# Five of eleven weight chunks of a down projection by seven block products in place of eight

## The chip, the core and the metric

The kernel runs on one core of one Trainium2 chip. The metric is the device time of one execution in microseconds (us), the median of several runs; lower is better. The core's engines are named as in the profile: PE is TensorE's matmul, PEld its weight load, DVE VectorE, ACT ScalarE, POOL GpSimd, SP the engine that issues most transfers. Each runs its own instructions in the order written, and waits where another has not finished.

## The reference

One decoder layer over 256 tokens of width 1024: two groups of attention heads, an output projection, a layer norm, a feed-forward block, a second layer norm. What matters here is the end of it, in float32:

```python
h = _layer_norm(ALPHA * h + mix_out, ln1_g[l], ln1_b[l])
gate = jnp.einsum('bsd,df->bsf', h, w_gate[l])
up = jnp.einsum('bsd,df->bsf', h, w_up[l])
ffn = jnp.einsum('bsf,fd->bsd', jax.nn.silu(gate) * up, w_down[l])
h = _layer_norm(ALPHA * h + ffn, ln2_g[l], ln2_b[l])
```

With `D_FF` = 2816, the down projection `w_down` is a product of 256 x 2816 by 2816 x 1024.

## The kernel before, in words

**Precision.** Every float32 operand of a big product is split in two parts of a type that TensorE takes in one pass: ACT copies the rounded high part, DVE subtracts it for the low part (`split`, L75). `prod` (L177) then issues three matmuls for one product: high by high, high by low, low by high. Nearly all matmuls and splits stand at L68, the helper that records them; the tile names tell them apart.

**Weights.** They come in chunks of 128 x 2048 (1 MB). The class `Weights` (L79) loads each with one transfer into a ring of four raw buffers (`wraw`) and splits it into a ring of `NSPLIT` = 5 pairs (`whi`, `wlo`). A chunk can be split once the matmuls that read the pair five places before are done. `piece` splits the next slice; `get` splits what is still missing of a chunk; `free` gives a pair back.

**Feed-forward.** 22 groups f of 128 features. From f = 3 on `ff_by_channel` (L566) issues 48 matmuls of 256 columns per group (tile `pg`), then ACT takes the silu of the gate half, DVE multiplies by the up half, and the product is split into the two tiles `a` that the down projection reads. Between the matmuls, `Order.fill` (L380) hands out a piece of 512 columns of the next weights each time its own count of time passes `PACE`.

**Down projection** (L605 to L641). Eleven chunks c of two feature groups each. The activations are stationary (128 x 128), the weights move. Token block t = 0 is summed in two banks of 512 columns, t = 1 in three, of 512, 256 and 256 columns (`thirds`), all named `d`. The first seven chunks go through all five banks one after the other: per chunk 18 matmuls of 512 columns and 12 of 256. After each, two pieces of 1024 columns of a later chunk are split. The last four chunks (`nlast`) are gone through bank by bank in `finish` (L631): first the two banks of t = 0, whose layer norm then runs on DVE, then the three of t = 1. `layer_norm` (L490) adds the residual `x_nat` times ALPHA to each bank, takes statistics, normalises and stores.

PSUM has eight banks, in four tags of two: `big`, `o`, `in`, `sml`. Neither rule of order is written by hand to the instruction: a scheduler orders each engine's instructions between what must wait for what.

Of the kernel before, what the change touches and what calls it, by code (L numbers as in the profile page):

```python
# [10 lines left out]
F32 = mybir.dt.float32  # L11
# [24 lines left out]
NWARM = 7  # L36
ALPHA = 2.0 ** 0.25
# [7 lines left out]
def decoder_layer(ctx: ExitStack, tc: tile.TileContext, first, x, wqk, wv, wo, wgu, wd,  # L45
# [33 lines left out]
    class Weights:  # L79


        def __init__(self, chunks):
            self.chunks = chunks
            self.raw, self.parts = [], []
            self.pos = 0
            self.freed = 0

        def load(self, n=NRAW):

            while len(self.raw) < min(n, len(self.chunks), len(self.parts) + NRAW - (self.pos % 2048 > 0)):  # L90
# [5 lines left out]

        def piece(self, width):

            c, o = divmod(self.pos, 2048)
            if c == len(self.chunks):  # L100
                return False
            if o == 0:
                if c - self.freed >= NSPLIT:
# [12 lines left out]
        def get(self, c, width=512):  # L116
            while self.pos < (c + 1) * 2048:
                assert self.piece(width)
            return self.parts[c]

        def free(self, c):
            self.freed = max(self.freed, c + 1)
# [37 lines left out]
    for h in range(2):  # L160
# [4 lines left out]
                       *(wo[c] for c in range(4)), *(wgu[f] for f in range(NFF)), *(wd[c] for c in range(NFF // 2))])  # L165
# [193 lines left out]
    class Order:  # L359
        def __init__(self):  # L360
            self.now = 0.0
            self.steps = []
            self.since = 0.0

# [19 lines left out]
        def fill(self, cost, fn):  # L384
# [4 lines left out]
            while self.since >= PACE:  # L389
                self.since -= PACE  # L390
# [99 lines left out]
    def layer_norm(acc, res, g, b, dst, after, pieces, after_pieces=None):  # L490
# [4 lines left out]
        for i, c in enumerate(pieces):  # L495
            nc.vector.scalar_tensor_tensor(y[:, c], res[:, c], ALPHA, acc[i][:, :c.stop - c.start],
# [69 lines left out]
    def ff_by_channel(f, tag):  # L566
        w = weights.get(14 + f, 1024)
        act_tiles(f)
        p = bank(tag, "pg")
        for half in range(2):  # L570
            for kt in range(KT):
                c = slice(kt * 256 + half * 128, kt * 256 + half * 128 + 128)
                od.fill(0.33, lambda: prod(p[:, half * 256:half * 256 + 256], (w[0][:, c], w[1][:, c]),
                                           (xhi[:, kt, :], xlo[:, kt, :]), kt == 0, kt == KT - 1))
        weights.free(14 + f)
        a = gated(p[:, 0:256], p[:, 256:512], [128, 256], "aw")
        split(a, *act[f])
# [22 lines left out]
    for f in range(NX, NFF):  # L600
        ff_by_channel(f, ("in", "sml")[f % 2])
# [6 lines left out]
    accd = [[bank(tag, f"d{t}") for tag in tags] for t, tags in enumerate((("big", "big"), ("o", "sml", "in")))]  # L608

    def down(t, f, i, w):  # L610
        tk = slice(t * 128, t * 128 + 128)
        p = pieces[t][i]
        c = slice((f % 2) * 1024 + p.start, (f % 2) * 1024 + p.stop)
        ah, al = act[f]
        prod(accd[t][i][:, :p.stop - p.start], (ah[:, tk], al[:, tk]), (w[0][:, c], w[1][:, c]),
             f == 0, f == NFF - 1)
# [94 lines left out]
```

## Time and profile before

| | us |
|---|---|
| median of 3 runs (lowest, highest) | 322.66 (322.24, 324.42) |
| the profiled execution | 322.32 |
| its span, first to last instruction | 320.6 |
| PE busy in the span | 310.2 (97%) |
| DVE busy | 206.1 (64%) |
| ACT busy | 176.6 (55%) |
| down projection, matmuls on the chain that ended last | 61.23 |

The span is what the trace covers; the execution's own time is 1.7 us longer. Matmul rows overlap in the trace, since each is shown from its start to its modelled end: the rate of TensorE is read from the distance between starts, not from the length of a row. In a timeline, a row with x2 stands for two instructions merged.

### The profile page before, as it was taken

Reading aid. Unit: us, or ns where it says so; the run is one execution under the profiler, and the core shown is the slowest. Engines: PE = TensorE matmul, PEld = TensorE weight load, DVE = VectorE, ACT = ScalarE, POOL = GpSimd, SP = SyncE. Lnnn points to the kernel's source line nnn. Section 1 sums busy time; section 2 is a strip of 40 time slices with the busy share of each in tenths; the row PEclk is TensorE's granted clock in tenths of the full one; section 3 lists DMA queues with packets and bytes.
Section 4 is the critical chain, followed back from the end, with each engine's and each line's share of the span. In section 5 each row is a group of like instructions: output and inputs, shape, how many; then the busy total and the mean of one; then the engine's idle time right before and its main releaser. Section 6 shows DMA issues by size and latency. Waiting matters only on the chain.

```text
span 320.6 us, 5490 instructions
## 1 busy us (share of the span) xinstructions
PE 310.2 (97%) x2175; PEld 283.3 (88%) x2175; DVE 206.1 (64%) x422; ACT 176.6 (55%) x385; POOL 4.1 (1%) x20
## 2 busy tenths in 40 slices
PE   7999999999999999999999999999999999999990
PEld 4988898799987778999999999999999988888890
DVE  3878998669887389998465464655635534350455
ACT  5789997777787367575364553635535542430000
POOL 5000000000000000000000000000000000000000
PEclk9999999999999999999999999999999999999996
DMA  7989877297333003779563554645445464000011
GB/s 238 376 320 377 274 273 271 103 376 280 133 133 123 10 0 131 261 283 372 153 246 133 214 181 159 237 139 216 171 169 226 142 245 139 3 0 0 2 65 65
DMA packets 9946, 58.03 MB, mean 181 GB/s; under 512 B 1216, under 2 KB 1856, under 8 KB 3648
## 3 DMA queue, kind: packets, MB, share of 16 engines
q1 hardware_dynamic: 9632, 57.22, 49.2%
q10 hardware_dynamic: 288, 0.46, 0.4%
q8 instruction: 17, 0.28, 0.3%
q14 instruction: 9, 0.07, 0.1%
HBM read 56.63 MB, written 1.05 MB: 180 GB/s over the span
## 4 chain that ended last, share of the span: by engine, by line
PE 92%; DMA 3%; DVE 2%; ACT 1%; issue 0%; SPq 0%; DVEq 0%
PE pg L68 39%; PE d L68 19%; PE p_in L68 18%; PE acc L68 7%; DMA wraw<-in_wv 2%; PE z L68 2%; PE o L324 1%; PE s L68 1%; DMA wraw<-in_first 1%; PE z L265 1%; PE o L329 1%; PE tr L524 1%; PE o L342 1%; SPq L132 0%; DVE y L512 0%
## 5 line engine op out<-in xcount | busy, mean ns | idle before, releaser
L68 DVE TENSOR_TENSOR wlo<-wraw,whi 128x512 fp32r<-128x512 f32 (+2 forms) x184 | 127.5, 721 | 72.4 <-ACT whi L68 71.8
L68 ACT ACTIVATE whi<-wraw 128x512 fp32r<-128x512 f32 (+2 forms) x184 | 113.4, 655 | 80.0 <-PE pg L68 47.9
L68 PE MATMUL pg<-xhi,whi 128*128 128x256 f32 x304 | 85.5, 281 | 0.0
L68 PE MATMUL pg<-xhi,wlo 128*128 128x256 f32 x304 | 85.4, 281 | 0.0
L68 PE MATMUL pg<-xlo,whi 128*128 128x256 f32 x304 | 85.4, 281 | 0.0
L68 PEld LDWEIGHTS pg<-xlo,whi 128*128 128x128 f32 x304 | 57.4, 189 | 0.0
L68 PEld LDWEIGHTS pg<-xhi,whi 128*128 128x128 f32 x304 | 57.3, 189 | 0.0
L68 PEld LDWEIGHTS pg<-xhi,wlo 128*128 128x128 f32 x304 | 57.3, 189 | 0.0
L68 PE MATMUL d<-whi,a 128*128 128x512 f32 (+1 forms) x220 | 56.7, 348 | 0.0
L68 PEld LDWEIGHTS d<-whi,a 128*128 128x128 f32 x220 | 38.3, 188 | 5.8
L68 PE MATMUL d<-wlo,a 128*128 128x512 f32 (+1 forms) x110 | 38.3, 348 | 0.0
L68 PE MATMUL p_in<-xhi,whi 128*128 128x256 f32 x128 | 36.9, 288 | 1.0 <-ACT whi L68 1.0
L68 PE MATMUL p_in<-xhi,wlo 128*128 128x256 f32 x128 | 36.3, 283 | 0.0
L68 PE MATMUL p_in<-xlo,whi 128*128 128x256 f32 x128 | 36.2, 282 | 0.0
L68 PEld LDWEIGHTS p_in<-xhi,whi 128*128 128x128 f32 x128 | 24.4, 190 | 2.7 <-ACT whi L68 1.8
L68 PEld LDWEIGHTS p_in<-xlo,whi 128*128 128x128 f32 x128 | 24.4, 191 | 0.2
L68 PEld LDWEIGHTS p_in<-xhi,wlo 128*128 128x128 f32 x128 | 24.3, 190 | 0.2
L68 PEld LDWEIGHTS d<-wlo,a 128*128 128x128 f32 x110 | 20.7, 189 | 2.8
L502 ACT ACTIVATE rs<-mv,eps_ln 128x1 f32<-128x1 f32 x4 | 1.2, 290 | 27.3 <-DVE mv L500 27.3
L68 PE MATMUL pg<-wlo,xhi 128*128 128x256 f32 x48 | 13.6, 286 | 0.0
L68 PE MATMUL pg<-whi,xhi 128*128 128x256 f32 x48 | 13.6, 286 | 0.0
L68 PE MATMUL p_in<-whi,xhi 128*128 128x512 f32 x32 | 13.2, 412 | 0.2 <-DVE ol L68 0.2
(126 smaller groups left out, 401.2 us busy)
## 6 DMA issues: line engine op xcount, KB each, us to landing
wraw<-in_wgu SPq DMA_DIRECT2D x22, 1024.0 KB, 4.8
wraw<-in_wd SPq DMA_DIRECT2D x11, 1024.0 KB, 4.8
wraw<-in_wqk SPq DMA_DIRECT2D x6, 1024.0 KB, 5.6
wraw<-in_wo SPq DMA_DIRECT2D x4, 1024.0 KB, 4.8
wraw<-in_wv SPq DMA_DIRECT2D x3, 1024.0 KB, 5.4
wraw<-in_first SPq DMA_DIRECT2D x7, 384.0 KB, 5.7
rows<-in_lnrows SPq DMA_DIRECT2D x2, 1024.0 KB, 6.9
wraw<-in_wv SPq DMA_DIRECT2D x2, 512.0 KB, 6.8
```

The lines of the kernel that those rows point to most:

```text
L68: return lambda *a, **k: tc.keep_in_program_order(f(*a, **k)) if Pinned.on else f(*a, **k)
L265: nc.tensor.matmul(dst, lhs, rhs, start=False, stop=True, skip_group_check=True)
L324: nc.tensor.matmul(o[r, 0:256], vt[g, 0][:, c], w0[:, h * 256:h * 256 + 256], start=True, stop=False, skip_group_check=True)
L329: nc.tensor.matmul(o[r, 128:256], vt[g, 1][:, c], w1[:, h * 128:h * 128 + 128], start=False, stop=True, skip_group_check=True)
L342: nc.tensor.matmul(ms, blkr, sq[:, i, :], start=i == 0, stop=i == 1, skip_group_check=True)
L502: nc.scalar.activation(r[:, 0:1], mv[:, 1:2], AF.Ln, bias=eps_ln)
L524: nc.tensor.transpose(p[:, i * 128:i * 128 + 128], h[:, kt * 128:kt * 128 + 128], ident)
```

## The change

Five chunks, c = 4 to 8 (`FAST`), go by seven block products. Each such chunk is a product of a 2 x 2 block matrix of activations (two token blocks by two feature groups, 128 x 128 each) and one of weights (two feature groups by two column halves, 128 x 512 each). Eight block products become seven of block sums, each into a PSUM bank of its own (`d1` to `d7`).

- The activations of two feature groups are written unsplit to a tile `slots` of eight blocks; four sums of 128 columns follow on DVE (`fast_sums`), and one split of seven blocks (896 columns, tiles `s`).
- The weights take two pairs of the ring (`unit`). The first pair holds three raw blocks split as before (the fourth is not filled). Then three subtractions on DVE, of 1024, 512 and 512 columns, write four block sums over the raw chunk in place, and these are split into the second pair.
- The chunks go in the order `DOWN`. The first seven are now 4, 5, 0, 6, 1, 7, 8; the ordinary ones among them (0 and 1) go into four banks of 512 columns, `d2`, `d3`, `d4` and `d8`.
- Before the last four chunks (2, 3, 9, 10) the banks that the outputs share (`d1`, `d5`, `d6`, `d7`, and the right half of `d8`) are added into the residual `x_nat`, with one ACT copy and ten DVE instructions. The last four then end in `d2`, `d3`, `d4`, the left half of `d8` and a new bank `d9` that takes the place of `d1`.
- From f = 14 on `PACE` is 0.9 in place of 1.39; and the scratch of the program's dynamic transfers is set to 1024.

```diff
+DOWN = (4, 5, 0, 6, 1, 7, 8, 2, 3, 9, 10)
+FAST = (4, 5, 6, 7, 8)
...
+        def unit(self):
+            self.taken += 1
+            return tuple(wp.tile([128, 2048], F32R, tag=tag, name=tag, bufs=NSPLIT) for tag in ("whi", "wlo"))
+
+        def full(self):
+            return self.taken - self.freed >= NSPLIT
...
+            if self.at == 0:
+                if self.full():
                     return False
                 self.load(c + 1)
-                self.parts.append(tuple(wp.tile([128, 2048], F32R, tag=tag, name=tag, bufs=NSPLIT)
-                                        for tag in ("whi", "wlo")))
-            hi, lo = self.parts[c]
-            k = slice(o, o + width)
-            split(self.raw[c][:, k], hi[:, k], lo[:, k])
-            self.pos += width
-            if self.pos % 2048 == 0:
+                self.parts.append([self.unit()])
+            if c in self.fast:
+                if not self.sums(c):
+                    return False
...
+        def sums(self, c):
+
+            r = self.raw[c]
+            parts = self.parts[c]
+            if self.at == 0:
+                for k in (slice(0, 512), slice(1024, 2048)):
+                    split(r[:, k], parts[0][0][:, k], parts[0][1][:, k])
+                self.at = 512
+            elif self.at == 512:
+                b = r.rearrange("p (i n) -> p i n", i=4)
+                nc.vector.tensor_sub(b[:, 0:2, :], b[:, 1:4:2, :], b[:, 0:2, :])
+                nc.vector.tensor_sub(b[:, 3, :], b[:, 3, :], b[:, 0, :])
+                nc.vector.tensor_sub(b[:, 2, :], b[:, 2, :], b[:, 3, :])
+                self.at = 1024
+            else:
+                if self.at == 1024:
+                    if self.full():
+                        return False
+                    parts.append(self.unit())
+                o = (self.at - 1024) * 2
+                k = slice(o, o + 1024)
+                split(r[:, k], parts[1][0][:, k], parts[1][1][:, k])
+                self.at += 512
+            return True
...
-            while self.since >= PACE:
-                self.since -= PACE
+            while self.since >= self.pace:
+                self.since -= self.pace
...
+    def fast_sums(c):
+        q = slots.pop(c)
+        nc.vector.tensor_add(q[:, 3, :], q[:, 7, :], q[:, 2, :])
+        nc.vector.tensor_sub(q[:, 4, :], q[:, 3, :], q[:, 0, :])
+        nc.vector.tensor_sub(q[:, 5, :], q[:, 0, :], q[:, 7, :])
+        nc.vector.tensor_sub(q[:, 6, :], q[:, 1, :], q[:, 4, :])
+        fast_act[c] = tuple(ff.tile([128, 7, 128], F32R, name=f"s{i}{c}", bufs=1) for i in range(2))
+        split(q[:, 0:7, :], *fast_act[c])
...
+        if f == NFF - 8:
+            od.pace = 0.9
...
-    accd = [[bank(tag, f"d{t}") for tag in tags] for t, tags in enumerate((("big", "big"), ("o", "sml", "in")))]
+    pr = {i: bank(tag, f"d{i}") for i, tag in ((1, "big"), (2, "big"), (3, "o"), (4, "o"), (5, "in"), (7, "sml"),
+                                                (6, "in"), (8, "sml"))}
+
+    fast_ops = ((1, 0, 0, 0), (2, 1, 0, 1024), (3, 6, 0, 1536), (4, 2, 1, 1024), (5, 3, 1, 0), (7, 5, 1, 512),
+                (6, 4, 1, 1536))
...
-    for c in range(NFF // 2 - nlast):
-        w = weights.get(base + c, 1024)
-        for f in (2 * c, 2 * c + 1):
-            for t in range(2):
-                for i in range(len(pieces[t])):
-                    down(t, f, i, w)
-        weights.free(base + c)
-        weights.piece(1024)
-        weights.piece(1024)
-    wl = {c: weights.get(base + c, 1024) for c in range(NFF // 2 - nlast, NFF // 2)}
+    for n, c in enumerate(DOWN[:-nlast]):
+        w = weights.get(base + n, 1024)
+        if c in FAST:
+            sh, sl = fast_act[c]
+            for i, k, u, o in fast_ops:
+                add(i, pr[i], (sh[:, k, :], sl[:, k, :]), (w[u][0][:, o:o + 512], w[u][1][:, o:o + 512]))
+        else:
+            for f in (2 * c, 2 * c + 1):
+                for i, t, k in ((2, 0, halves[0]), (3, 0, halves[1]), (4, 1, halves[0]), (8, 1, halves[1])):
+                    down(t, f, i, pr[i], k, w)
+        weights.free(base + n)
+        while weights.piece(1024):
+            pass
+    nc.scalar.activation(u2, pr[1], AF.Copy)
+    onto(res[0][0], res[0][0], ALPHA, pr[1])
+    nc.vector.tensor_add(u2, u2, pr[6])
+    onto(res[0][1], res[0][1], ALPHA, u2)
+    nc.vector.tensor_add(u3, u2, pr[7])
+    nc.vector.tensor_add(res[0][1], res[0][1], pr[5])
+    onto(res[1][0], res[1][0], ALPHA, u3)
+    onto(res[1][1], res[1][1], ALPHA, u3)
+    nc.vector.tensor_add(res[1][1], res[1][1], pr[5])
+    nc.vector.tensor_add(res[1][1][:, 256:512], res[1][1][:, 256:512], pr[8][:, 256:512])
+
+    wl = {c: weights.get(base + len(DOWN) - nlast + n, 1024) for n, c in enumerate(DOWN[-nlast:])}
+    pr[9] = bank("big", "d9")
+    last_acc = (((2, pr[2]), (3, pr[3])), ((4, pr[4]), (8, pr[8][:, 0:256]), (9, pr[9][:, 0:256])))
...
```

The helper at L68 stands at L71 in the changed kernel; `L144` to `L146` are the three subtractions on the weights. What moves is seen at three places.

**TensorE, the first chunk of the down projection.** Before, the rows of one feature group of chunk 0 (`a00`, `a10` its activations' high and low parts; the group has 15 such rows):

```order
L68 MATMUL d0_3070<-whi_3008,a00_1539 128x512
L68 MATMUL d0_3070<-wlo_3009,a00_1539 128x512
L68 MATMUL d0_3070<-whi_3008,a10_1540 128x512
L68 MATMUL d0_3071<-whi_3008,a00_1539 128x512
L68 MATMUL d0_3071<-wlo_3009,a00_1539 128x512
L68 MATMUL d0_3071<-whi_3008,a10_1540 128x512
L68 MATMUL d1_3072<-whi_3008,a00_1539 128x512
L68 MATMUL d1_3072<-wlo_3009,a00_1539 128x512
L68 MATMUL d1_3072<-whi_3008,a10_1540 128x512
L68 MATMUL d1_3073<-whi_3008,a00_1539 128x256
L68 MATMUL d1_3073<-wlo_3009,a00_1539 128x256
L68 MATMUL d1_3073<-whi_3008,a10_1540 128x256
```

Now, from the same place, the start of chunk 4 (`s04` and `s14` its seven blocks, high and low):

```order
L71 MATMUL d1_3097<-whi_2866,s04_2254 128x512
L71 MATMUL d1_3097<-wlo_2867,s04_2254 128x512
L71 MATMUL d1_3097<-whi_2866,s14_2255 128x512
L71 MATMUL d2_3098<-whi_2866,s04_2254 128x512
L71 MATMUL d2_3098<-wlo_2867,s04_2254 128x512
L71 MATMUL d2_3098<-whi_2866,s14_2255 128x512
```

A chunk of this kind is seven such triples, 21 matmuls, all of 512 columns; before it was 30, of which 12 had 256. The program has 57 matmuls fewer.

**ScalarE, after the last feature group.** Before, behind the change of its function table, each pair of rows is one whole chunk:

```order
L603 ACT_TABLE_LOAD
L68 ACTIVATE whi_3257<-wraw_3111 128x1024 x2
L68 ACTIVATE whi_3295<-wraw_3149 128x1024 x2
L68 ACTIVATE whi_3333<-wraw_3187 128x1024 x2
L68 ACTIVATE whi_3339<-wraw_3225 128x1024 x2
L68 ACTIVATE whi_3345<-wraw_3263 128x1024 x2
L68 ACTIVATE whi_3351<-wraw_3301 128x1024 x2
```

Now (`wraw_2855` is chunk 6, `wraw_2922` chunk 1, `wraw_3051` chunk 7, `wraw_3132` chunk 8):

```order
L679 ACT_TABLE_LOAD
L71 ACTIVATE whi_3134<-wraw_2855 128x1024
L71 ACTIVATE whi_3143<-wraw_2855 128x1024
L71 ACTIVATE whi_3172<-wraw_2922 128x1024 x2
L71 ACTIVATE whi_3180<-wraw_3051 128x512
L71 ACTIVATE whi_3180<-wraw_3051 128x1024
L71 ACTIVATE whi_3143<-wraw_2855 128x1024
L71 ACTIVATE whi_3213<-wraw_3051 128x1024
L71 ACTIVATE whi_3242<-wraw_3132 128x512
```

The last piece of chunk 6 (second row of `whi_3143`) stands behind chunk 1 and behind the first pair of chunk 7.

**VectorE, the last splits and the first layer norm.** Before, the last split is followed at once by the norm:

```order
L68 TENSOR_TENSOR wlo_3346<-wraw_3263,whi_3345 128x1024 x2
L68 TENSOR_TENSOR wlo_3352<-wraw_3301,whi_3351 128x1024 x2
L496 SCALAR_TENSOR_TENSOR y_3406<-x_nat_897,d0_3070 128x512
L498 BN_STATS bst_3405<-y_3406 128x6
L496 SCALAR_TENSOR_TENSOR y_3406<-x_nat_897,d0_3071 128x512
```

Now (`wraw_3219` is chunk 9, `wraw_3257` chunk 10; L543 is the norm's first instruction):

```order
L71 TENSOR_TENSOR wlo_3317<-wraw_3219,whi_3316 128x1024 x2
L728 SCALAR_TENSOR_TENSOR x_nat_897<-x_nat_897,d1_3097 128x512
L71 TENSOR_TENSOR wlo_3344<-wraw_3257,whi_3343 128x1024 x2
L732 TENSOR_TENSOR y_3349<-y_3349,d6_3103 128x512
L728 SCALAR_TENSOR_TENSOR x_nat_897<-x_nat_897,y_3349 128x512
L734 TENSOR_TENSOR y_3349<-y_3349,d7_3102 128x512
L735 TENSOR_TENSOR x_nat_897<-x_nat_897,d5_3101 128x512
L728 SCALAR_TENSOR_TENSOR x_nat_897<-x_nat_897,y_3349 128x512 x2
L543 SCALAR_TENSOR_TENSOR y_3410<-x_nat_897,d2_3098 128x512
L738 TENSOR_TENSOR x_nat_897<-x_nat_897,d5_3101 128x512
L545 BN_STATS bst_3409<-y_3410 128x6
L739 TENSOR_TENSOR x_nat_897<-x_nat_897,d8_3104 128x256
```

The additions into the residual stand between the splits and the norm, one of them ahead of the last split, two behind the norm's first instruction.

## Rows read from the trace of the kernel before

**Rows 1.** The page: busy time (us), share of the span, instructions of each engine
```profile
PE 310.2 (97%) x2175; PEld 283.3 (88%) x2175; DVE 206.1 (64%) x422; ACT 176.6 (55%) x385; POOL 4.1 (1%) x20
```

**Rows 2.** Longest of the four waits of TensorE's matmuls: us in total, times, longest us
```profile
PE warm L140 <- DVE idle L137: 1.1, 1, 1.1
```

**Rows 3.** Chain that ended last: start us, us, what; down projection and the last link
```profile
251.44 61.23 PE d L68 x330
...
315.83 0.75 DVE y L512
```

**Rows 4.** Timeline, TensorE, down projection's start: start us, us (of merged instructions), what
```profile
251.28 0.39 PE L68 MATMUL d<-whi,a 128*128 128x512 f32 x1
...
254.28 0.40 PE L68 MATMUL d<-wlo,a 128*128 128x512 f32 x1
...
256.23 0.28 PE L68 MATMUL d<-wlo,a 128*128 128x256 f32 x1
...
256.59 0.28 PE L68 MATMUL d<-wlo,a 128*128 128x256 f32 x1
...
257.06 0.40 PE L68 MATMUL d<-wlo,a 128*128 128x512 f32 x1
```

**Rows 5.** Timeline, TensorE, token block 1 of the last four chunks
```profile
298.88 0.40 PE L68 MATMUL d<-wlo,a 128*128 128x512 f32 x1
...
306.58 0.39 PE L68 MATMUL d<-wlo,a 128*128 128x512 f32 x1
...
307.17 0.28 PE L68 MATMUL d<-wlo,a 128*128 128x256 f32 x1
...
312.27 0.28 PE L68 MATMUL d<-wlo,a 128*128 128x256 f32 x1
```

**Rows 6.** Timeline, TensorE, output projection: 512 columns into two banks in turn
```profile
102.06 0.40 PE L68 MATMUL acc<-whi,mh 128*128 128x512 f32 x1
...
103.89 0.39 PE L68 MATMUL acc<-whi,ml 128*128 128x512 f32 x1
...
105.93 0.39 PE L68 MATMUL acc<-whi,ml 128*128 128x512 f32 x1
```

**Rows 7.** Timeline, VectorE, feed-forward into down projection and the last norms
```profile
218.79 1.29 DVE L68 TENSOR_TENSOR wlo<-wraw,whi 128x512 fp32r<-128x512 f32 x2
...
252.46 1.23 DVE L68 TENSOR_TENSOR wlo<-wraw,whi 128x1024 fp32r<-128x1024 f32 x1 [2.67 <-ACT whi L68]
253.60 0.41 DVE L545 TENSOR_TENSOR silu<-silu,pg 128x256 f32<-128x256 f32 x1
...
255.06 0.42 DVE L68 TENSOR_TENSOR a<-silu,a 128x256 fp32r<-128x256 f32 x1
258.12 2.36 DVE L68 TENSOR_TENSOR wlo<-wraw,whi 128x1024 fp32r<-128x1024 f32 x2 [2.64 <-ACT whi L68]
...
296.05 0.69 DVE L496 SCALAR_TENSOR_TENSOR y<-x_nat,d 128x512 f32<-128x512 f32 x1 [7.72 <-PE d L68]
296.77 0.69 DVE L498 BATCH_NORM_STATS2 bst<-y 128x6 f32<-128x512 f32 x1
...
303.41 1.41 DVE L507 SCALAR_TENSOR_TENSOR y<-y,mv,rows 128x512 f32<-128x512 f32 x2
```

**Rows 8.** Timeline, ScalarE, same stretch
```profile
251.36 1.06 ACT L68 ACTIVATE whi<-wraw 128x1024 fp32r<-128x1024 f32 x1 [2.60 <-PE pg L68]
...
254.48 1.28 ACT L603 ACT_TABLE_LOAD   x1
257.03 2.01 ACT L68 ACTIVATE whi<-wraw 128x1024 fp32r<-128x1024 f32 x2 [1.26 <-PE d L68]
```

**Rows 9.** Group of 128 columns on VectorE, 60 to 150 us: count, busy us, mean ns, idle before
```profile
L563 DVE TENSOR_TENSOR a<-pt,a 128x128 fp32r<-128x128 f32 x6 | 1.7, 286 | 0.1
```

**Rows 10.** Window in the feed-forward: length, busy us (x instructions) of each engine, clock, DMA share
```profile
180.00:200.00 20.00, 20.00 (x171) 20.00 (x170) 10.65 (x21) 8.39 (x19) 0.00 (x0) 1.00 0.48 165
```

**Rows 11.** The page's DMA issues: line, count, KB each, us from issue to landing
```profile
wraw<-in_wd SPq DMA_DIRECT2D x11, 1024.0 KB, 4.8
```

More of the change, by code (lines that the diff above doesn't have):

```diff
@@ L79, in decoder_layer, with __init__ @@
     class Weights:
-        def __init__(self, chunks):
+        def __init__(self, chunks, fast):
             self.chunks = chunks
+            self.fast = fast
             self.raw, self.parts = [], []
-            self.pos = 0
-            self.freed = 0
+            self.done = 0
+            self.at = 0
+            self.taken = self.freed = self.behind = 0
         def load(self, n=NRAW):
-            while len(self.raw) < min(n, len(self.chunks), len(self.parts) + NRAW - (self.pos % 2048 > 0)):
+            while len(self.raw) < min(n, len(self.chunks), len(self.parts) + NRAW - (self.at > 0)):
                 raw = wp.tile([128, 2048], F32, tag="wraw", name="wraw", bufs=NRAW)
@@ L116, in get @@
         def get(self, c, width=512):
[L117 removed]
+            while self.done <= c:
                 assert self.piece(width)
[L119 removed]
+            return self.parts[c] if c in self.fast else self.parts[c][0]
         def free(self, c):
[L122 removed]
+            while self.behind <= c:
+                self.freed += 2 if self.behind in self.fast else 1
+                self.behind += 1
     xhi = cst.tile([128, KT, S], F32R, name="xhi")
@@ L488, in decoder_layer, with layer_norm @@
     pieces = (halves, thirds)
-    def layer_norm(acc, res, g, b, dst, after, pieces, after_pieces=None):
+    def layer_norm(acc, res, g, b, dst, after, pieces, after_pieces=None, scale=ALPHA):
         st = ff.tile([128, len(pieces), 6], F32, tag="bst", name="bst", bufs=2)
@@ L567, in ff_by_channel @@
         w = weights.get(14 + f, 1024)
-        act_tiles(f)
+        c, odd = divmod(f, 2)
+        fast = c in FAST
+        if not fast:
+            act_tiles(f)
+        elif not odd:
+            slots[c] = ff.tile([128, 8, 128], F32, tag="slots", name="slots", bufs=1)
         p = bank(tag, "pg")
@@ L611, in down, with add @@
+    begun = set()
+    def add(i, dst, lhs, rhs):
+        prod(dst, lhs, rhs, i not in begun, False)
+        begun.add(i)
+    def down(t, f, i, dst, cols, w):
         tk = slice(t * 128, t * 128 + 128)
-        p = pieces[t][i]
-        c = slice((f % 2) * 1024 + p.start, (f % 2) * 1024 + p.stop)
+        c = slice((f % 2) * 1024 + cols.start, (f % 2) * 1024 + cols.stop)
         ah, al = act[f]
-        prod(accd[t][i][:, :p.stop - p.start], (ah[:, tk], al[:, tk]), (w[0][:, c], w[1][:, c]),
-             f == 0, f == NFF - 1)
+        add(i, dst, (ah[:, tk], al[:, tk]), (w[0][:, c], w[1][:, c]))
@@ new lines, in decoder_layer, with onto @@
+    res = [[x_nat[:, t, k] for k in halves] for t in range(2)]
+    y = ff.tile([128, D], F32, tag="y", name="y", bufs=2)
+    u2, u3 = y[:, halves[0]], y[:, halves[1]]
+    def onto(dst, a, scale, b):
+        nc.vector.scalar_tensor_tensor(dst, a, scale, b, op0=ALU.mult, op1=ALU.add)
+    nc.scalar.activation(u2, pr[1], AF.Copy)
[3 more added lines that the diff above has]
+    nc.vector.tensor_add(u3, u2, pr[7])
@@ L631, in finish @@
     def finish(t):
-        for i in range(len(pieces[t])):
+        for cols, (i, dst) in zip(pieces[t], last_acc[t]):
             for c in wl:
                 for f in (2 * c, 2 * c + 1):
-                    down(t, f, i, wl[c])
+                    down(t, f, i, dst, cols, wl[c])
         def store(c, yo):
@@ L639, in store @@
             queue.dma_start(out[t * 128:t * 128 + 128, c], yo[:, c])
-        layer_norm(accd[t], x_nat[:, t, :], rows2[:, 0, :], rows2[:, 1, :], None, store, pieces[t],
-                   (halves, (slice(0, 512), slice(512, 896), slice(896, 1024)))[t])
+        layer_norm([dst for _, dst in last_acc[t]], x_nat[:, t, :], rows2[:, 0, :], rows2[:, 1, :], None, store,
+                   pieces[t], (halves, (slice(0, 512), slice(512, 896), slice(896, 1024)))[t], 1.0)
     finish(0)
```

45 lines of the change are left out of this document (31 added, 14 removed).

## The prediction

> **What bounds the kernel now.** I read the page's busy line first: TensorE is busy 97% of the span, VectorE 64%, ScalarE 55% [rows 1]. Then TensorE's waits: four in all, the longest 1.1 us, at the very start [rows 2]. Then the chain that ended last: the down projection lies on it whole, 61.23 us of matmuls without a break, and after it only the last norm on VectorE [rows 3]. So time is saved here by giving TensorE less to do, and lost by making it wait. I call the first matmul of the down projection T = 0 (251.28 us [rows 4]).
>
> TensorE's price is the distance between starts. One feature group of the old order (9 matmuls of 512 columns, 6 of 256) takes 257.06 - 254.28 = 2.78 us, a chunk 5.56, seven chunks 38.9. In it a matmul of 256 costs 0.36 / 3 = 0.12 (256.23 to 256.59, one triple), which leaves (2.78 - 0.72) / 9 = 0.229 for one of 512 [rows 4]. Two other prices of 512 stand in the trace. 33 steps in one bank (298.88 to 306.58) give 0.2333; there a 256 costs 5.10 / 45 = 0.113 [rows 5]. Triples that change between two banks, with nothing narrower among them, give 3.87 / 17 = 0.2276, and 2.04 / 9 = 0.2267 over the last nine [rows 6].
>
> **What the change takes from TensorE.** The new first seven chunks are triples of 512 columns that change bank after every triple, which is nearest to [rows 6]. I take 0.2276, with 0.2267 and 0.2333 as ends. A chunk by block products is 21 x 0.2276 = 4.78, an ordinary one 24 x 0.2276 = 5.46; five and two make 34.8. Against 38.9 that saves **4.1 us** (4.2 and 3.2 at the ends). The ordinary ones gain only 0.1 each, by wider pieces. The last four chunks keep their matmuls and banks' widths (22.2 us), and the tail behind the last matmul its instructions.
>
> The Trainium skill (TensorE: Matmul & The Clock Gate, section Back-to-back issue gap) gives N / 2.4 + 2.5 ns between starts, 216 ns for 512 columns and 109 for 256; by that an old chunk is 5.19, a new one 4.53, an ordinary one 5.18, and the saving 3.3. The rows are above it at both widths, so the sum doesn't use it.
>
> **What it adds to VectorE and ScalarE, in the feed-forward.** For two feature groups: four sums of 128 columns at 0.29 [rows 9], and one subtraction of 896 columns (1.03, by 7/8 of half of 2.36) for two of 0.42 [rows 7]: +1.3 us in 11.2. VectorE is busy 10.65 of 20 us there [rows 10], so it fits. If it did not, TensorE would first feel it when a bank of `pg` isn't read out; there are four, one per group of 48 x 20 / 171 = 5.6 us. I cost this at nothing. ScalarE's copies change by a few tenths. The faster hand-out of pieces from f = 14 gets ahead only until the ring of five pairs is full.
>
> **What it adds to the weights.** A chunk by block products is split over 3584 columns, not 2048. VectorE: 0.65 for the 512 (half of 1.29) and 3 x 1.18 (half of 2.36) [rows 7], 4.2 us. The three subtractions in place, 1024, 512 and 512 columns, each waiting for the one before, are not in the trace. Below: the split's own subtraction without waits, 1.18 + 0.65 + 0.65 = 2.5. Above: the norm's in-place instruction, 1.41 / 2 = 0.71 per 512 columns, doubled for 1024, plus 0.03 to the next that depends on it (296.05 + 0.69 to 296.77) [rows 7], 2.9. I take 2.7, since the shape is the split's and the waits are real. So 6.9 us of VectorE per such chunk, where TensorE takes 4.78, and 2.36 per ordinary one, where it takes 5.46. The alternation of the two kinds and the pairs split before T = 0 must carry the difference. Splitting begins when a pair is free.
>
> Before T = 0: the first pairs of chunk 5 come free at -11.2 and -5.6. VectorE then has 0.65 + 2.7 + 1.18 and one group's 0.83, done by -5.9; then ScalarE's 1.05 ahead of 2.36 + 0.83, done by about -1.3. Chunks 4 and 5 are ready.
>
> From T = 0 (TensorE ends chunk 4 at 4.8, 5 at 9.6, 0 at 15.0, 6 at 19.8, 1 at 25.3, 7 at 30.0, 8 at 34.8; of a chunk by block products the first pair is read out 2.05 after its start):
> - Chunk 0 waits for f = 21, so begins at 0.1 on ScalarE and 1.2 on VectorE [rows 7, 8]; with f = 21's own work it ends at 4.4.
> - Then VectorE has the first part of 6, chunk 1, the 512 of chunk 7 and the last piece of 6, in that order: 6.9 + 2.36 + 0.65 = 9.9, to 14.3. ScalarE reaches that last piece only behind chunk 7's first pair, which waits for chunk 5's second (9.6), and has it by 12.5. TensorE needs it at 15.0 + 2.05 = 17.1.
> - The rest of 7, with the 512 of 8 among it, 6.9: 21.2, needed 25.3. The rest of 8, 6.2: 27.4, needed 30.0.
> - Chunks 2 and 3: 32.1, needed 34.8. Chunk 9: its pair comes free at 30.0, VectorE has it at 34.5. One addition into the residual, 0.69, then chunk 10: its two halves at 36.4 and 37.6. The first bank of the last four comes to it at 34.8 + 18 x 0.2333 = 39.0, to its second half at 39.7.
>
> So TensorE waits nowhere, and VectorE is 2.1 to 2.6 us early at the tightest place, after 33 us with hardly a gap. ScalarE, at 2.01 per 2048 columns and 1.28 for its table [rows 8], has the shorter queue.
>
> Transfers take 4.8 us [rows 11] and a raw buffer is now held until its sums are split: chunk 8 lands at 9.2 for a need at 17, chunk 10, behind chunk 8's buffer, at 27.4 + 4.8 = 32.2 for a need on VectorE at 35.2. Hidden.
>
> **The additions into the residual.** After chunk 10, six instructions of 0.7: 37.6 to 41.8. The norm's first instruction, due at 34.8 + 5.6 = 40.4, is 1.4 late, but with three more small ones VectorE is through by 44.5, and the norm's next is due at 46.0. Nothing reaches the end. Bank `d9` needs its old content read by 35.2 and is first written near 54; the right half of `d8` is read by 44.5, and its left half written from 51.6. Nothing is moved across the queue that issues transfers.
>
> **Sum.** The profiled execution is 322.32 us, its span 320.6 and 1.7 outside; less 4.1 that is 318.2. The median of the runs is 0.34 above the profiled one: **318.6 us**, 1.3% less.
>
> **Rivals.**
> - *VectorE's long queue runs late.* For it: 33 us almost without a gap, in which each subtraction needs ScalarE's result first, and 6.9 us of work under 4.78 of matmuls. Against: the pair timings taken already hold that wait. It decides from 2.1 to 2.6 us of lateness, 7%. At 15% (5.0) TensorE waits 2.9 before chunk 10, and 1.2 of the gain is left: 321.5. The Trainium skill (same page, the table at its head) gives VectorE and ScalarE a strict first-in-first-out queue: what is late holds up all behind it. The prediction's order of waits agrees with that; no row here tests it.
> - *Slower: the subtractions in place cost double.* Place: three instructions per chunk on VectorE, source and target the same tile. At 5.4 instead of 2.7, chunks 4 and 5 take up the idle time before T = 0 (2 x 2.7), chunk 0 ends about 1 later, and chunks 6, 7, 8 add 8.1, so chunk 10 comes at 46.7 against 39.7: TensorE waits 7.0 and loses 2.9 net, **325.5**. It turns the result from about 1.8 times on, where the wait is 4.1. Against: the norm's in-place row is 0.71 for 512 columns against 0.69 for one that isn't.
> - *512 columns keep the price of one bank.* At 0.2333 a matmul the 153 take 35.7, the saving is 3.2 and the time 319.5. For it: 33 steps without an exception [rows 5]. Against: no triple stays in its bank here, as in [rows 6]. The skill's spacing, above, would come out nearly the same.
> - *It doesn't shorten TensorE's work.* 57 matmuls fewer (5 x 9 + 2 x 6) are in the program, so only a wider price per matmul could do that: 38.9 / 153 = 0.254, above every row. 322.7.
>
> **Chances.** Forecast 0.68 (318.0 to 319.4: prices from 0.2267 to 0.230, and 0.4 of scatter), late queue 0.13 (319.5 to 322.5), the price of one bank 0.09, double subtractions 0.08, no gain 0.02. The range from 317.8 to 321.0 leaves out the slow case, no gain and half of the late queue, 0.16 or so. What counts as a change is 1%, 3.2 us, about what a measurement of this kernel can tell: faster takes nearly all of the forecast, half of the price of one bank and a little of the late queue, 0.69; slower half of the double subtractions, 0.04; the rest is within, 0.27.
>
> **What will show it.** The down projection's matmuls on the chain should be 61.2 - 4.1 = 57.1 us long, 273 of them. The distance from a chunk's first matmul to the next should be 4.8 and 5.5. VectorE's subtractions on `wraw` should be 1.2 and 0.7 us, with hardly an idle stretch from 3 to 37 us after T = 0, and no wait of TensorE on ScalarE or VectorE before chunk 10. Wrong would be the forecast if such a wait is there, if 512 columns cost 0.233 with changing banks, or if the matmuls of `pg` begin to wait from f = 8 on.

## The result, and the profile after

The changed kernel takes **319.09 us** (median of 4 runs, 318.06 to 319.48), the kernel before in the same comparison 323.35 (4 runs, 322.24 to 324.42): ratio 0.988, 95% interval 0.984 to 0.992. It is faster, by about as much as forecast (318.6). The profiled executions are 318.06 against 322.32 us, their spans 316.3 against 320.6. Medians and ratios here and below leave out three executions that ran far longer: two of the kernel before in the comparison of e1 to e4 (382.7 and 783.3 us), one of e6 (507.7).

The page's busy line answers to [rows 1]: TensorE has 57 matmuls fewer and 4.1 us less to do, VectorE 47 instructions and 32 us more. That this 4.1 is also the forecast's saving is chance: 1.2 of it lie in the feed-forward, as the chain below shows.

```profile
PE 306.1 (97%) x2118; PEld 277.8 (88%) x2118; DVE 237.8 (75%) x469; ACT 186.2 (59%) x389; POOL 4.1 (1%) x20
```

All waits of TensorE's matmuls (columns as in [rows 2]). They are four, none of them in the feed-forward or in the down projection, so all that VectorE does more lies beside TensorE's work:

```profile
PE warm L185 <- DVE idle L182: 1.0, 1, 1.0
PE p_in L71 <- ACT whi L71: 0.9, 1, 0.9
PE o L370 <- ACT w L359: 0.2, 1, 0.2
PE p_in L71 <- DVE ol L71: 0.2, 1, 0.2
```

The chain that ended last, feed-forward, down projection and last link (columns as in [rows 3]):

```profile
146.81 103.84 PE pg L71 x885
250.65 57.78 PE d L71 x273
...
311.58 0.75 DVE y L559
```

The down projection took 61.23 [rows 3] and takes 57.78: **3.45 us less**, where 4.1 was forecast. The feed-forward's link was 105.02 before and is 103.84 here. That 1.2 us belongs to the execution and not to the change, as the experiments show; the stages ahead of it ended 0.4 us later. So the difference of the profiles, 4.3, is 3.45 of change and 0.8 of chance.

Where the 0.6 us of the forecast's 4.1 went is read from TensorE's timeline, at the second matmul of each of the seven chunks and of the last four (start, us, what; T = 0 is 250.49):

```profile
250.73 0.39 PE L71 MATMUL d<-wlo,s 128*128 128x512 f32 x1
...
255.62 0.39 PE L71 MATMUL d<-wlo,s 128*128 128x512 f32 x1
...
260.53 0.39 PE L71 MATMUL d<-wlo,a 128*128 128x512 f32 x1
...
266.00 0.39 PE L71 MATMUL d<-wlo,s 128*128 128x512 f32 x1
...
270.89 0.40 PE L71 MATMUL d<-wlo,a 128*128 128x512 f32 x1
...
276.35 0.39 PE L71 MATMUL d<-wlo,s 128*128 128x512 f32 x1
...
281.25 0.40 PE L71 MATMUL d<-wlo,s 128*128 128x512 f32 x1
...
286.14 0.39 PE L71 MATMUL d<-wlo,a 128*128 128x512 f32 x1
```

Chunks 0 and 1 (`a`) take 5.47 and 5.46, as forecast: 0.228 us a matmul. The five chunks by block products (`s`) take 4.89 to 4.91, not 4.78: 4.90 / 21 = 0.2333. All seven are 286.14 - 250.73 = 35.41, where 34.8 was forecast, and 5 x 21 x (0.2333 - 0.2276) = 0.60 is the whole difference. From the first matmul of the last four (285.91) to the last matmul (308.13) it is 22.2, as forecast.

VectorE's timeline, one chunk's three subtractions, then the last splits with the additions into the residual and the first norm (in brackets the idle time before, and what ended it):

```profile
272.01 1.22 DVE L144 TENSOR_TENSOR wraw<-wraw 128x1024 f32<-128x1024 f32 x1
273.26 0.69 DVE L145 TENSOR_TENSOR wraw<-wraw 128x512 f32<-128x512 f32 x1
273.99 0.69 DVE L146 TENSOR_TENSOR wraw<-wraw 128x512 f32<-128x512 f32 x1
274.60 2.44 DVE L71 TENSOR_TENSOR wlo<-wraw,whi 128x1024 fp32r<-128x1024 f32 x2
...
284.64 0.68 DVE L728 SCALAR_TENSOR_TENSOR x_nat<-x_nat,d 128x512 f32<-128x512 f32 x1
285.24 2.35 DVE L71 TENSOR_TENSOR wlo<-wraw,whi 128x1024 fp32r<-128x1024 f32 x2
...
290.03 1.28 DVE L728 SCALAR_TENSOR_TENSOR x_nat<-x_nat,y 128x512 f32<-128x512 f32 x2
291.66 0.69 DVE L543 SCALAR_TENSOR_TENSOR y<-x_nat,d 128x512 f32<-128x512 f32 x1 [0.35 <-PE d L71]
...
297.21 0.69 DVE L543 SCALAR_TENSOR_TENSOR y<-x_nat,d 128x512 f32<-128x512 f32 x1 [3.34 <-PE d L71]
```

The subtractions take 274.60 - 272.01 = 2.6 us in a row. The last split ends at 287.59, T + 37.1 (forecast 37.6). The norm's first instruction even waited 0.35 us for TensorE, and the second 3.34: the additions into the residual are hidden.

In the feed-forward the window that answers to [rows 10] has VectorE at 12.68 us of 20, 2.0 more, which is 1.1 in the 11.2 us of two groups (forecast 1.3), and TensorE busy throughout:

```profile
180.00:200.00 20.00, 20.00 (x173) 20.00 (x172) 12.68 (x26) 9.41 (x18) 0.00 (x0) 1.00 0.48 165
```

### The profile page after: what moved, and what is told of

It is laid out like the page before. It is cut to its first block, busy times and chain, and to the rows that moved or that the text cites. A ratio compares the mean times of both kernels' runs of the same rounds, so it can differ in the third digit from the quotient of the medians.

```text
span 316.3 us, 5436 instructions
## 1 busy us (share of the span) xinstructions
PE 306.1 (97%) x2118; PEld 277.8 (88%) x2118; DVE 237.8 (75%) x469; ACT 186.2 (59%) x389; POOL 4.1 (1%) x20
## 4 chain that ended last, share of the span: by engine, by line
PE 91%; DMA 3%; DVE 2%; ACT 1%; issue 0%; SPq 0%; DVEq 0%
PE pg L71 39%; PE d L71 18%; PE p_in L71 18%; PE acc L71 7%; DMA wraw<-in_wv 2%; PE z L71 2%; DMA wraw<-in_first 2%; PE o L370 1%; PE s L71 1%; PE z L311 1%; PE o L375 1%; PE tr L571 1%; PE o L388 1%; SPq L177 0%; DVE wlo L71 0%
## 5 line engine op out<-in xcount | busy, mean ns | idle before, releaser
L71 DVE TENSOR_TENSOR wlo<-wraw,whi 128x512 fp32r<-128x512 f32 (+2 forms) x192 | 136.6, 737 | 38.8 <-ACT whi L71 37.8
L71 ACT ACTIVATE whi<-wraw 128x512 fp32r<-128x512 f32 (+2 forms) x192 | 120.2, 669 | 59.7 <-PE pg L71 37.2
L71 PE MATMUL pg<-xhi,whi 128*128 128x256 f32 x304 | 85.2, 280 | 0.0
L71 PE MATMUL pg<-xlo,whi 128*128 128x256 f32 x304 | 85.0, 280 | 0.0
L71 PE MATMUL pg<-xhi,wlo 128*128 128x256 f32 x304 | 85.0, 280 | 0.0
L71 PEld LDWEIGHTS pg<-xlo,whi 128*128 128x128 f32 x304 | 57.1, 188 | 0.0
L71 PEld LDWEIGHTS pg<-xhi,whi 128*128 128x128 f32 x304 | 57.1, 188 | 0.0
L71 PEld LDWEIGHTS pg<-xhi,wlo 128*128 128x128 f32 x304 | 57.1, 188 | 0.0
L71 PE MATMUL p_in<-xhi,whi 128*128 128x256 f32 x128 | 37.1, 290 | 0.9 <-ACT whi L71 0.9
L71 PE MATMUL p_in<-xlo,whi 128*128 128x256 f32 x128 | 36.4, 285 | 0.0
L71 PE MATMUL p_in<-xhi,wlo 128*128 128x256 f32 x128 | 36.4, 285 | 0.0
L71 PE MATMUL d<-whi,a 128*128 128x512 f32 (+1 forms) x112 | 31.0, 360 | 0.0
L71 PEld LDWEIGHTS p_in<-xhi,whi 128*128 128x128 f32 x128 | 24.6, 192 | 2.8 <-ACT whi L71 1.9
L71 PEld LDWEIGHTS p_in<-xlo,whi 128*128 128x128 f32 x128 | 24.7, 193 | 0.2
L71 PEld LDWEIGHTS p_in<-xhi,wlo 128*128 128x128 f32 x128 | 24.6, 192 | 0.1
L71 PEld LDWEIGHTS d<-whi,a 128*128 128x128 f32 x112 | 20.0, 189 | 3.4
L71 PE MATMUL d<-whi,s 128*128 128x512 f32 x70 | 22.5, 395 | 0.0
L71 PE MATMUL d<-wlo,a 128*128 128x512 f32 (+1 forms) x56 | 20.2, 360 | 0.0
L71 PEld LDWEIGHTS d<-whi,s 128*128 128x128 f32 x70 | 13.1, 188 | 3.1
L71 PE MATMUL d<-wlo,s 128*128 128x512 f32 x35 | 13.8, 395 | 0.0
L71 PE MATMUL pg<-wlo,xhi 128*128 128x256 f32 x48 | 13.6, 286 | 0.0
```

Source lines behind the costliest of these rows:

```text
L71: return lambda *a, **k: tc.keep_in_program_order(f(*a, **k)) if Pinned.on else f(*a, **k)
```

## Experiments

Two questions were open: why 512 columns cost 0.2333 us in some chunks and 0.2276 in others, and whether VectorE's longer queue was as near to holding TensorE back as the prediction had it. A third was whether the feed-forward's 1.2 us belong to the change.

**e1_scratch: the tiles' addresses alone.** The changed kernel also reserves less room for DMA descriptors, which moves all tiles down by 15,360 bytes. The kernel before, with that one edit:

```diff
-    nc = bacc.Bacc("TRN2", target_bir_lowering=False, num_devices=1)
+    nc = bacc.Bacc("TRN2", target_bir_lowering=False, num_devices=1, dynamic_dma_scratch_size=1024)
```

> The kernel before, with nothing changed but the scratch of the dynamic transfers (16384 bytes per partition down to 1024), which moves every tile in SBUF down by 15360 bytes. The changed kernel's feed-forward took 103.8 us on the chain for 105.0 (5.63 us per feature group for 5.70, from the first group on, where nothing else differs yet). Theory 'place': the price of a 256-column matmul there depends on where the tiles lie, so this kernel's groups take 5.63 us too, its feed-forward 1.2 us less, its span 319.4 for 320.6, ratio 0.996. Rival 'run to run' or 'the changed work': groups of 5.70 and a span of 320.6 as before, ratio 1.000.

321.97 us (10 runs) against 322.13 (11 runs), ratio 0.9997 (0.997 to 1.002); the feed-forward's 19 last groups 108.42 us (before 108.46), the down projection 61.10 from first to last matmul, as before. So this shift, a multiple of 512 bytes, does nothing, to the feed-forward or to anything else.

**e2_pad_ff: the offset of the stationary tiles.** 64 bytes put in front of the `s` tiles:

```diff
+    ff.tile([128, 16], F32, name="pad", bufs=1)
     slots = {}
```

> The changed kernel, with an unused tile of 64 bytes per partition ahead of the tiles that the block products' activations stand in, so that these (and the activations of f = 18 to 21) begin 64 bytes later. In the changed kernel a matmul of 512 columns costs 0.2333 us where its stationary tile begins 32 bytes past a multiple of 128, and 0.2276 where it begins 96 past one. Theory 'offset': the offset of the stationary tile sets the price; chunks by block products fall from 4.90 to 4.78, five of them by 0.6 us, with f = 18 to 21 some 0.8 us in all, span 315.5 for 316.3. Rival 'kind': the price belongs to the chunks of this kind (a stationary block used for one bank only); they stay at 4.90 and the span at 316.3.

318.22 us (4 runs), ratio 0.988 (0.982 to 0.995). Chunks by block products take 4.87 to 4.89 us, 0.02 less than without the pad, so the offset that this run tried isn't the reason: the `s` tiles now begin 96 bytes past a multiple of 128, as the cheap tiles do. Past a multiple of 512 it is 352 bytes, against 288 without the pad and 480 for the cheap tiles, and no run tried that last value in `ff`. The feed-forward's groups took 108.43 us, as in the kernel before.

**e3_run: the five chunks in a row.** Without ordinary chunks between them, in which VectorE catches up:

```diff
-DOWN = (4, 5, 0, 6, 1, 7, 8, 2, 3, 9, 10)
+DOWN = (4, 5, 6, 7, 8, 0, 1, 2, 3, 9, 10)
```

> The changed kernel with its five chunks by block products one after the other (order 4, 5, 6, 7, 8, 0, 1, 2, 3, 9, 10) in place of 4, 5, 0, 6, 1, 7, 8. Theory: such a chunk asks 6.9 us of VectorE and 4.9 of TensorE, and the ordinary chunks between them pay the difference. In a row, the second pair of chunk 8 comes at 22.7 us after the down projection's start and is wanted at 21.7: TensorE waits there once, for 1.1 us (0.5 to 2), and the time is some 1.1 us above the changed kernel's (span 317.4 for 316.3). Rival: the order doesn't matter since the ring of five pairs carries enough; no wait, same span within 0.3.

318.48 us (4 runs), ratio 0.988 (0.983 to 0.993), the down projection 57.73 on the chain, and no wait: the expected 1.1 us did not come. Every chunk by block products took 4.90, so the price doesn't come from the alternation either. In the program TensorE's order had changed inside chunk 8 (block products into `d4` and `d7` begun, `d5` whole between them), just where the late piece would have been waited for.

**e4_double: VectorE's work on a chunk raised by four subtractions.** The slower rival, with its price put in by hand (the results go to a part of `wlo` that nothing reads):

```diff
                 nc.vector.tensor_sub(b[:, 2, :], b[:, 2, :], b[:, 3, :])
+                for i in range(4):
+                    nc.vector.tensor_sub(parts[0][1][:, 512:1024], b[:, i, :], b[:, 3 - i, :])
```

> The changed kernel with VectorE's work on the block sums of the weights about doubled: four more subtractions of 512 columns per chunk by block products, into a part of the split tiles that nothing reads (2.6 us per chunk). It plays the slower rival of the prediction, that the subtractions cost twice what was assumed. Expected by the prediction's schedule: after the down projection's start 7.8 us more on VectorE, of which 2.5 are slack; TensorE waits some 5 us in all before the last four chunks are done, the span is about 321 to 322 for 316.3, and the gain over the kernel before is gone. Rival: VectorE has more room than the schedule says, and the span grows by less than 2 us.

318.94 us (one run). TensorE waits nowhere in the down projection, which is as long as in the changed kernel (57.78 on the chain), although VectorE's last two splits end 6.2 us later after T = 0 than in the changed kernel (294.35 - 251.04 = 43.3, against 37.1):

```profile
251.20 57.76 PE d L71 x273
```

```profile
291.99 2.36 DVE L71 TENSOR_TENSOR wlo<-wraw,whi 128x1024 fp32r<-128x1024 f32 x2
```

Two things took up the 12 us (20 subtractions, 0.6 from start to start). Idle time of VectorE, before T = 0 and in its short gaps, took some 6 of them. For the rest, TensorE's order in the program came out differently: thirteen matmuls of `d3`, on chunks that were ready, stand ahead of the first that needs the low part of chunk 10. In the changed kernel that one starts at T + 39.8, here at T + 42.8, 0.6 after its split has ended (T + 42.1). The scheduler had put matmuls of the next bank where the wait would have been.

**e7_eight: raised by eight.** The same edit with eight subtractions.

> Eight more subtractions of 512 columns on VectorE in each chunk by block products (results into an unused part of `wlo`), 5.2 us per chunk, 26 us in all, on top of the changed kernel. With four more TensorE did not wait, and chunk 10 was split at T + 43.3. Now chunk 10 should be split between T + 50 and T + 57. Theory 'TensorE's order gives way': the last four chunks take 22.2 us from T + 35.4, and only a quarter of them, 5.5 us, needs chunk 10, so TensorE waits only from T + 52 on: 0 to 5 us, 319 to 324. Rival 'fixed order' (the slower case of the prediction): chunk 10 is wanted at T + 39.6, TensorE waits 10 us or more, 329 or more.

326.91 us (one run): past what reordering can cover, by 2.9 more than the upper end of that theory. TensorE's first long wait is not at chunk 10 but in the second half of chunk 8 (start, us, what, the idle time before):

```profile
284.52 0.73 PE L71 MATMUL d<-whi,s 128*128 128x512 f32 x2 [1.31 <-ACT whi L71]
285.47 0.73 PE L71 MATMUL d<-whi,a 128*128 128x512 f32 x2 [0.23 <-ACT whi L71]
287.37 0.73 PE L71 MATMUL d<-whi,s 128*128 128x512 f32 x2 [1.16 <-ACT whi L71]
289.32 0.80 PE L71 MATMUL d<-wlo,s 128*128 128x512 f32 x1 [1.23 <-DVE wlo L71]
...
290.34 0.63 PE L71 MATMUL d<-wlo,s 128*128 128x512 f32 x1
290.77 0.63 PE L71 MATMUL d<-whi,s 128*128 128x512 f32 x1
```

The windows of TensorE (length, busy us and instructions, granted clock, DMA share, GB/s) show what followed:

```profile
280.00:284.00 4.00, 3.21 (x14) 1.00 0.00 0
284.00:289.30 5.30, 2.19 (x6) 0.89 0.21 29
289.30:294.60 5.30, 5.28 (x12) 0.50 0.42 173
294.60:300.00 5.40, 5.40 (x24) 0.97 0.55 194
```

After a stretch with 2.19 us of work in 5.3, the granted clock stands at 0.50, the lower of its two levels, for 5.3 us: a matmul steps by 0.43 us (290.34 to 290.77) instead of 0.23, and twelve of them cost 2.3 us on top of the waits. From T = 0 to the last matmul it is 65.3 us, 7.7 more than in the changed kernel. So the slower rival's mechanism exists, from somewhere between four and eight subtractions more per chunk, and the clock makes it cost more than its waits alone.

**e5_low: the place of the stationary tiles.** Within single traces one difference ran through: matmuls whose stationary tiles lie in the pool `cst`, at low addresses of a partition (they begin at 20 to 51 KB), settled at 0.2267, those whose tiles lie in `ff` (165 to 212 KB) at 0.2333. The addresses here and below are those of the built programs, a KB being 1000 bytes. The `s` tiles of chunks 4 and 5 put into `cst`:

```diff
-        fast_act[c] = tuple(ff.tile([128, 7, 128], F32R, name=f"s{i}{c}", bufs=1) for i in range(2))
+        pool = cst if c in (4, 5) else ff
+        fast_act[c] = tuple(pool.tile([128, 7, 128], F32R, name=f"s{i}{c}", bufs=1) for i in range(2))
```

> The changed kernel with the s tiles of chunks 4 and 5 placed in the pool `cst` (low in each partition, beside the tiles of the mixed heads) and those of chunks 6, 7 and 8 left in `ff`. Theory 'place of the stationary tile': a triple whose stationary tiles lie low steps at 0.227 us a matmul, one whose tiles lie in `ff` at 0.2333; then chunks 4 and 5 take 21 x 0.2276 = 4.78 (4.90 before), 6, 7 and 8 stay at 4.90, and the down projection's matmuls are 0.24 us shorter. Rival 'the stream itself' (seven banks in turn, seven stationary pairs): all five stay at 4.87 to 4.90. Either way the time is 318 to 319.

TensorE's timeline, the second matmul of chunks 4, 5, 0, 6 and 1:

```profile
251.32 0.40 PE L71 MATMUL d<-wlo,s 128*128 128x512 f32 x1
...
256.09 0.39 PE L71 MATMUL d<-wlo,s 128*128 128x512 f32 x1
...
260.85 0.39 PE L71 MATMUL d<-wlo,a 128*128 128x512 f32 x1
...
266.29 0.39 PE L71 MATMUL d<-wlo,s 128*128 128x512 f32 x1
...
271.19 0.40 PE L71 MATMUL d<-wlo,a 128*128 128x512 f32 x1
```

Chunks 4 and 5 take 4.77 and 4.76 now, 0.2267 a matmul; chunk 6, left in `ff`, still 4.90. Same instructions, same order of banks, another place: another height, and with it 480 bytes past a multiple of 512 in place of 288. The down projection is 57.48 on the chain, 0.3 less, and 317.73 us (6 runs) the lowest of the medians, ratio 0.986 (0.982 to 0.989). Against e8's interval, below, that is no difference that the times alone could show.

**e6_three and e10_three: block products for three chunks only.** The other direction: chunks 7 and 8 become ordinary, but with activations in `ff`.

```diff
-FAST = (4, 5, 6, 7, 8)
+FAST = (4, 5, 6)
```

> The changed kernel with block products for chunks 4, 5 and 6 alone; 7 and 8 are ordinary, their activations (feature groups 14 to 17) in `ff`. A chunk by block products should save 3 x 0.23 = 0.6 to 0.7 us, so the down projection's matmuls get longer by 1.1 if an ordinary chunk from `ff` costs 5.46 (theory 'the stream itself'), by 1.4 if the price follows the place of the stationary tiles (24 x 0.2333 = 5.60). If VectorE's queue had held TensorE back somewhere, less work for it would give some of that back. Forecast 319.1 + 1.1 to 1.4 = 320.2 to 320.5, ratio to the kernel before 0.991.

319.67 us (median of 7 runs), ratio 0.992 (0.990 to 0.995): 0.5 below the forecast's lower end and 1.1 above e8, which would be 0.55 for each chunk. The intervals are too wide to tell 1.1 from 1.4; e10 is the same kernel again, and its profile decides.

> Block products for chunks 4, 5 and 6 alone, once more, for a profile at the full clock. Chunks 7 and 8 are then ordinary, with the activations of groups 14 to 17 in `ff`, and 0 and 1 ordinary with theirs in `cst`. Theory 'place of the stationary tile': 24 x 0.2333 = 5.60 us for 7 and 8, 5.45 for 0 and 1. Rival 'the stream of the block products': 5.45 for all four. Time 319.7 (1.1 above the changed kernel's 318.6).

319.82 us (one run). TensorE's timeline, second matmul of chunks 1, 7, 8 and of the last four:

```profile
271.27 0.40 PE L71 MATMUL d<-wlo,a 128*128 128x512 f32 x1
...
276.73 0.39 PE L71 MATMUL d<-wlo,a 128*128 128x512 f32 x1
...
282.33 0.39 PE L71 MATMUL d<-wlo,a 128*128 128x512 f32 x1
...
287.93 0.39 PE L71 MATMUL d<-wlo,a 128*128 128x512 f32 x1
```

Chunk 1 (`cst`) takes 5.46, chunks 7 and 8 (`ff`) 5.60: 24 x 0.2333. These are ordinary chunks, so it isn't the stream of block products. The down projection is 59.17 on the chain, 1.40 more than in the changed kernel, as 2 x (5.60 - 4.90) says.

**e11_mixed: a high and a low tile in one triple.** The high parts of chunks 4 to 7 in `cst`, their low parts in `ff`:

```diff
+        fast_act[c] = tuple((cst if i == 0 and c < 8 else ff).tile([128, 7, 128], F32R, name=f"s{i}{c}", bufs=1)
+                            for i in range(2))
```

> The changed kernel with the high parts of the s tiles of chunks 4, 5, 6 and 7 in `cst` and their low parts in `ff`; chunk 8 wholly in `ff`. In a triple two matmuls then have a low stationary tile and one a high one. Theory 'each matmul by its own tile': 21 steps of 0.2289 on average, 4.81 us for chunks 4 to 7, and 4.90 for 8. Rival 'the stream settles only if all tiles lie low' (the steps needed about five matmuls to settle at 0.2267): 4.87 to 4.90 for all. Time 318.2 to 318.6.

317.09 us (one run). The four chunks take 4.87, 4.85, 4.85 and 4.85, chunk 8 4.90: between the two theories. In a settled triple the two matmuls with the low tile step by 0.228 to 0.229, the one with the high tile by 0.236. It looks as if each were paid by its own tile and something were lost at each change of place; no run separates the two. The time is 1.1 below the forecast; the profile's feed-forward was 1.2 us short (see e8).

**e9_pace: the faster hand-out of pieces undone.**

```diff
-        if f == NFF - 8:
-            od.pace = 0.9
```

> The changed kernel with the old rate of handing out weight pieces (1.39) kept to the end of the feed-forward: the faster hand-out from group 14 on undone. Prediction's theory: the ring of five pairs is full either way, so nothing changes: the down projection's matmuls 57.6 us, no wait of TensorE, time 318.6 plus or minus 1. Rival: chunks 4, 5 or 0 are split too late and TensorE waits at T = 0 to T + 10, 1 to 4 us more.

318.77 us (one run), the down projection 57.64 from first to last matmul, as in e8, no wait. This part of the change does nothing to the time.

**e8_again: the changed kernel, more runs.** Nothing edited.

> The changed kernel again, nothing altered. In the first profiles the down projection was 3.46 us shorter and the feed-forward 1.2 us shorter, which it was in no other variant. If that was run to run, the profile shows 108.4 or 107.2 us of feed-forward by chance, and the median of many runs stands 3.5 (3.0 to 4.3) below the kernel before: ratio 0.987 to 0.991. If the change shortens the feed-forward as well, 107.2 again and ratio 0.985 to 0.986.

318.56 us (6 runs) against 322.05 (15 runs): **3.5 us, ratio 0.988 (0.985 to 0.992)**. Its chain, and the same link of e11's:

```profile
146.08 105.02 PE pg L71 x885
251.11 57.77 PE d L71 x273
```

```profile
146.03 103.84 PE pg L71 x885
```

The same kernel now shows 105.02 us of feed-forward, and e11, which changes nothing there, 103.84. The other profiles at full clock that have this link whole show 105.02 or 105.03, the first of the changed kernel 103.84. e7's link is broken by its waits, but from the first of the 19 groups to T = 0 it takes 107.24 us, as do e11 and the first profile; the other nine, e6 aside, take 108.42 to 108.46. So the 1.2 us come and go between executions of one and the same kernel (the first profile and e8). The kernel before and e1, one profile each, both show the longer time; whether the old kernel has the shorter one too isn't shown. The down projection's 3.5 is in every profile of the changed kernel.

## Why the prediction was right, and where it was off

- **The bound and the mechanism: right.** TensorE's matmuls set the end, 57 fewer of them shorten the chain by their price, and what they cost elsewhere is hidden. The chain's link of the down projection shows it alone, and e6 and e10 confirm it per chunk.
- **The saving: 3.45 instead of 4.1.** The mis-sized term is the price of 512 columns in the block products, taken as 0.2276 "nearest to [rows 6]" because the bank changes after every triple. It measured 0.2333, the prediction's own upper end. That 512 columns cost 0.233 with changing banks is one of the three signs of being wrong that the prediction named; it came true in five of the seven chunks and cost 0.6 us, which the stated range holds. The bank has nothing to do with it: [rows 6] have their stationary tiles in `cst`, [rows 5] in `ff`, and the number of banks was taken for the cause. e5 and e10 turn the price with the pool, in both directions. The measured saving of 3.45 is nearer to the 3.2 of the rival "512 columns keep the price of one bank" than to the forecast. That rival was right in number for five of the seven chunks, by a wrong reason, and wrong for chunks 0 and 1. The changed kernel's last four chunks show the two prices inside one bank, which takes chunks 2 and 3 (`cst`) and then 9 and 10 (`ff`): three steps from 287.53 take 0.68, or 0.227 each, and six from 289.60 take 1.40, or 0.2333 (TensorE's timeline).

```profile
287.53 0.39 PE L71 MATMUL d<-wlo,a 128*128 128x512 f32 x1
...
288.21 0.39 PE L71 MATMUL d<-wlo,a 128*128 128x512 f32 x1
...
289.60 0.40 PE L71 MATMUL d<-wlo,a 128*128 128x512 f32 x1
...
291.00 0.40 PE L71 MATMUL d<-wlo,a 128*128 128x512 f32 x1
```

- **What could have shown it.** In the old order all groups change banks alike; 0 to 7 have their tiles in `cst`, 8 to 13 in `ff`. From the first to the third `wlo` triple's start it is 254.28 [rows 4] to 255.66 in group 1 and 287.70 to 289.10 in group 13 (TensorE's timeline, kernel before):

```profile
255.66 0.39 PE L68 MATMUL d<-wlo,a 128*128 128x512 f32 x1
...
287.70 0.39 PE L68 MATMUL d<-wlo,a 128*128 128x512 f32 x1
...
289.10 0.39 PE L68 MATMUL d<-wlo,a 128*128 128x512 f32 x1
```

  Six steps of 512 columns: 1.38, or 0.230 each, against 1.40, or 0.2333. Whole groups hid it, since both take 2.78: at 256 columns it is the other way round, 0.12 in [rows 4] (`cst`) and 0.113 in [rows 5] (`ff`).
- **The median came out nearer than the sum.** 322.66 less the 3.45 measured is 319.2, and 319.09 was measured. That the comparison's own difference, 323.35 - 319.09 = 4.3, looks like the forecast's 4.1 is chance; over 6 and 15 runs it is 3.5 (e8).
- **VectorE's queue: right.** Subtractions 2.6 us (forecast 2.7), last split at T + 37.1 (37.6), no wait of TensorE, the additions into the residual just in time.
- **The late queue and the doubled subtractions: the mechanism is real, the price was wrong.** The prediction took 7.0 us of waiting for doubled subtractions. With nearly that much work added (e4) TensorE waited 0. Two steps failed: chunk 10 came at T + 43.3 and not 46.7, since idle time took up more; and the order of TensorE's matmuls was taken as fixed, while the built program has other matmuls where the wait would have been. Where it can't any more (e7), the first wait is in chunk 8, not at chunk 10, and half of the clock is lost for 5.3 us as well.
- **Hand-out of pieces: costed at nothing, and nothing it was** (e9).

The Trainium skill (TensorE: Matmul & The Clock Gate, section Back-to-back issue gap) gives 216 ns for a single 512-column matmul behind another and some 131 ns sustained in a stream of loads and matmuls. The streams here, each matmul with its load, step by 226.7 or 233.3 ns; neither figure is met, and the measurement decides.

## What to carry to other kernels

Before a price per matmul is taken from a row, sort the rows by all that differs between them (bank, width, stationary tile, its pool and its address), and look for a pair in which only one thing does; here two feature groups of the old down projection, one with its tiles in `cst` and one in `ff`, would have done. Where a scheduler sets the order, a wait that is worked out in the old order was too long in all three runs that tested one (e3, e4, e7): the edit that makes something late also makes the scheduler move other work there, until none is left. And a stage that doesn't change between two kernels shows what a single pair of profiles is worth: take that off before the difference is explained.

## What the runs showed of the hardware

A float32 matmul of 512 columns costs 226.7 ns when its stationary tile stands in the pool `cst` (its tiles begin at 20 to 51 KB of the partition in these kernels) and 233.3 ns when it stands in `ff` (165 to 212 KB), 3%, with the same instructions in the same order (e5; e10 and e11 agree). What it is about the place isn't settled. "Low" is not the whole rule: in the value projection of the kernel before, whose stationary `xhi` and `xlo` fill 17 to 33 KB, heights at which the cheap tiles of the changed kernel lie (20 to 37 KB), the steps are 0.233 on average over this run of nine matmuls:

```profile
30.00 0.40 PE L68 MATMUL p_in<-whi,xhi 128*128 128x512 f32 x1
...
31.86 0.39 PE L68 MATMUL p_in<-whi,xlo 128*128 128x512 f32 x1
```

One rival was left untested. Every tile in `cst` that was cheap begins 480 bytes past a multiple of 512, the tiles in `ff` 288 (352 in e2, which gained 0.02 us in 4.9), `xhi` and `xlo` 128. This remainder fits all these rows, the value projection's too, while the height fits all but that one. The value projection differs from the down projection in more than the place (its weights, the work around it), so it speaks against the height without settling it. e1 moved everything by a multiple of 512, and e5, e10 and e11 changed height and remainder together. A tile of `ff` that begins 480 bytes past such a multiple would decide.

The feed-forward's two lengths, 105.02 and 103.84 us for the same 885 matmuls at a granted clock of 1.00, are unexplained as well: 1.1% of a stage, from its first group on, that the next execution may not repeat.
